# Turning the units' results by DMA in 16-bit halves, or by TensorE

## The chip, the cores and the metric

The kernel runs on one core of one Trainium2 chip. The metric is the device time of one execution in microseconds (us). Engines are named as the profile names them: PE (TensorE, the matrix engine), PEld (its weight loads), DVE (VectorE), ACT (ScalarE), POOL (GpSimd), SP (SyncE, which here only issues transfers). "SPq" is SP's queue of DMA issues. Every engine runs its instructions in the order in which they were written, and waits on semaphores for others.

## The reference

One layer of an encoder block on 2048 tokens of 1024 features, fp32 in and out:

```python
h = rms_norm(x, norm_gain)
qa, ka, va, qb, kb, vb, ga, gb, mg = split(h @ w_in)
ya = banded_attention(norm(qa) * scale, norm(ka), va, window 128, sink_a) * silu(ga)       # 8 heads of 64
yb = merge of 3 dilated groups (dilation 1, 4, 16; 8 heads of 64 each) * silu(gb)
merged = sigmoid(mg[0] + b[0]) * (ya @ w_branch_a) + sigmoid(mg[1] + b[1]) * (yb @ w_branch_b)
out = x + merged @ w_out
```

`ya` and `yb` have 512 columns each. The change concerns them after the attention, just ahead of the product with the SiLU gates.

## The kernel before, in words

Values that enter a matrix product are split in two fp16 parts (high and low) and multiplied in three products, so TensorE has three matmuls for each one of the mathematics.

**Input phase** (to about 105 us): x is normalised, split and transposed into `XH` and `XL` (features on partitions, tokens along the free dimension).

**Main phase** (about 105 to 1420 us): 14 units, 2 of kind A (4 query heads each) and 12 of kind B (2 heads of one of the three groups). A unit has 8 pairs of token blocks; the loop variable `t` counts pairs, and all offsets in the tables are in pairs (`t + 0.483` is about half a pair later). A pair's projection is two PSUM banks `pj` of 24 matmuls each (L699). ScalarE copies a bank out (`rw`, L716; `vt`, L725), VectorE reads the rest of the values (`vt`, L731), and with that the bank is free; there are two banks. Then come the norms (VectorE and POOL), a split, and a transposition by DMA into the keys' ring (`kq`, L784, on SPq). An attention item takes logits (L869), subtracts maxima (`pr`, L884 on VectorE), exponentiates (ACT), splits (`p`, L897 on ACT, L901 on VectorE), transposes the probabilities by DMA (`pt<-p`, L907 on SPq) and multiplies with the values (`pv`, L918); ScalarE copies the result out (L941, L946, L950). Between the projections stand the matmuls of the gate projections (L325).

**Merging.** When a quarter (512 tokens) of a chunk (128 columns of ya or yb) is complete, `a_merge` or `b_merge_q` writes it as `ya`, 128 tokens by 4 blocks by 128 columns in fp32, and makes a `YPart` of it. There are 8 chunks (0 to 3 from kind A, 4 to 7 from kind B) of 4 quarters, so 32 parts. A part

- `load`s the gate values `yo` from DRAM (L970),
- `turn`s the four 128x128 blocks of fp32 on TensorE, with the identity `idf` as moving operand, into the PSUM bank `pt` (L984),
- `gate`s: one VectorE instruction multiplies `pt`, a scale and `yo` (L991),
- takes the maximum (`top`, L996), and `store`s to DRAM (L999).

After quarter 3 the chunk's maximum goes over the partitions through a small matmul (`max1` to `max3`), which shares the bank `pt` with the weights' norm sums; `held` keeps the users of that bank apart.

**Last phase** (from about 1420 us): gate, branch and output projections, nearly TensorE alone.

**The order.** Nothing is reordered later. Each step is put in a heap under a planned time, `at(time, step)`, and steps are written out by rising time, so the tables of offsets (`Y_PART`, `NORM`, `LAGS`, ...) set each engine's order. `chain` runs a part's steps in their sequence and puts off one that returns False by 0.04.

Of the kernel before, what the change touches and what calls it, by code (L numbers as in the profile page):

```python
# [21 lines left out]
F32 = mybir.dt.float32  # L22
F16 = mybir.dt.float16
I32 = mybir.dt.int32
AF = mybir.ActivationFunctionType
OP = mybir.AluOpType
AX = mybir.AxisListType
# [33 lines left out]
NPAIR = 8 * NU  # L61
# [9 lines left out]
A_MERGE = (0.085, 0.258, 0.51, 0.671, 1.503, 0.761)  # L71
B_MERGE = (-0.037, 0.133, 0.333, 0.507, 0.665, 1.053)
Y_PART = (-0.097, 0.483, 0.709, 0.893, 0.943)
GATE = (-0.123, -0.064, 0.329)
W_STEP = (0.1, 0.465, 1.9, 0.445, 4.197, 0.146, 0.342)
W_MAX = (3.762, 3.892)
# [3 lines left out]
Y_FREE = 0.15  # L80
Y_MAX = (0.026, 0.815, 0.839)
# [28 lines left out]
XT_BUFS = 14  # L110
RING = 576
KQ_COPY = 0.45
V_SLOTS = 14
PT_BUFS = 4
N_BIAS_A = 384
N_BIAS_B = 256
# [2 lines left out]
def block_kernel(tc, x, w_units, w_gate, w_mrg, w_brn, w_out, w_bra, gain, qkg, sink, bias_a, bias_b, b_merge, out):  # L119
    nc = tc.nc  # L120
    V = nc.vector
    A = nc.scalar
# [7 lines left out]
    wp = es.enter_context(tc.tile_pool(name="wp", bufs=2))  # L130
    us = es.enter_context(tc.tile_pool(name="us", bufs=1))
    main = ExitStack()
    sm = main.enter_context(tc.tile_pool(name="sm", bufs=4))
    ubuf = us.tile([128, 192], F32, name="ubuf")
    ucount = [0]

    def ucol():
# [18 lines left out]
    def pow2(mx, name):  # L156
# [3 lines left out]
        p = sm.tile([128, 1], F32, name="pw_p")  # L160
        V.tensor_scalar(p[:].bitcast(I32), m[:].bitcast(I32), 0x7F800000, None, OP.bitwise_and)
        r = sm.tile([128, 1], F32, name="pw_r")
# [30 lines left out]
    held = [False, True]  # L193
# [10 lines left out]
    def norm_pow(ps):  # L204
# [5 lines left out]
        p = sm.tile([128, 1], F32, name="pw_p")  # L210
        V.tensor_scalar(p[:].bitcast(I32), m[:].bitcast(I32), -0.5, float(0x5F3759DF), OP.mult, OP.add)
        V.tensor_scalar(p[:].bitcast(I32), p[:].bitcast(I32), 0x7F800000, None, OP.bitwise_and)
        s = ucol()
# [5 lines left out]
    def w_square(u, i):  # L219
# [5 lines left out]
        c = slice(2 * i, 2 * i + 2)  # L225
        A.activation(wtiles[u][2][:, c, :n], raw[:, c, :n], AF.Square, accum_out=wtiles[u][3][:, i:i + 1])

# [11 lines left out]
    def w_hi(u, i):  # L239
        n = 384 if u < NU else 256  # L240
        raw, s, inv, wh, wl = wtiles[u]
        c = slice(2 * i, 2 * i + 2)
        A.activation(wh[:, c, :n], raw[:, c, :n], AF.Copy, scale=s[:])

# [20 lines left out]

    def rs_guess(a, n):

        y = sm.tile([128, 10], F32, name="rs_y")
        V.tensor_scalar(y[:, :n].bitcast(I32), a.bitcast(I32), -0.5, float(0x5F3759DF), OP.mult, OP.add)  # L269
        return y[:, :n]  # L270

    def rs_newton(a, yv, r, n, pool):

        t = sm.tile([128, 10], F32, name="rs_t")
        tv = t[:, :n]
        if pool:
            G.tensor_tensor(tv, yv, yv, OP.mult)  # L277
            G.tensor_tensor(tv, tv, a, OP.mult)
            G.tensor_scalar(r, tv, 0.375, -1.25, OP.mult, OP.add)
            G.tensor_tensor(r, r, tv, OP.mult)  # L280
            G.tensor_scalar(r, r, 1.875, None, OP.add)
            G.tensor_tensor(yv, r, yv, OP.mult)
            G.tensor_tensor(tv, yv, yv, OP.mult)
            G.tensor_tensor(tv, tv, a, OP.mult)
            G.tensor_scalar(tv, tv, -0.5, 1.5, OP.mult, OP.add)
            G.tensor_tensor(r, tv, yv, OP.mult)
# [58 lines left out]
    def g_square(c, i=None):  # L345
# [8 lines left out]
        k = i or 0  # L354
        A.activation(gh[:, v, :], raw[:, v, :], AF.Square, accum_out=sq[:, k:k + 1])

# [251 lines left out]
    wk = main.enter_context(tc.tile_pool(name="wk", bufs=2, reuse_waits="tile"))  # L608
# [69 lines left out]
    blocks = [0]  # L678
    vring = wk.tile([128, V_SLOTS, 2, 130], F16, name="vt", bufs=1)
    vfree = list(range(V_SLOTS))  # L680
    G.memset(vring[:, :, :, HD:HD + 1], 2.0 ** -14)

    class Pair:
# [55 lines left out]

        def stats(self):  # L740
            n = 2 * self.nh
            ss = sm.tile([128, 10], F32, name="qss")
            V.tensor_reduce(ss[:, :n], self.sq[:, :n * HD].rearrange("p (h e) -> p h e", e=HD), AX.X, OP.add)
            V.tensor_scalar(ss[:, :n], ss[:, :n], QKE / HD, self.un.eps[:], OP.mult, OP.add)
            self.ss = ss[:, :n], rs_guess(ss[:, :n], n)

        def newton(self):
            n = 2 * self.nh
            self.rr = sm.tile([128, 10], F32, name="qr")
            rs_newton(*self.ss, self.rr[:, :n], n, True)  # L750

        def scale(self):
# [208 lines left out]
    class YPart:  # L961
# [8 lines left out]
            nc.sync.dma_start(out=self.o[:], in_=gtd[self.chunk][:, 512 * self.q:512 * self.q + 512])  # L970

        def plan(self, t):
            steps = [(t + d, f) for d, f in zip(Y_PART, (self.load, self.turn, self.gate, self.top, self.store))]
            if self.q == 3:
                steps += [(t + Y_PART[3] + d, f) for d, f in zip(Y_MAX, (self.max1, self.max2, self.max3))]
            chain(steps)

        def turn(self):
            if held[0]:
                return False  # L980
            held[0] = True
            self.ps = pt_p.tile([128, 512], F32, name="pt")
            for b in range(4):
                T.transpose(self.ps[:, 128 * b:128 * b + 128], self.y[:, b, :], idf[:])  # L984

        def free(self):
            held[0] = False

        def gate(self):
            at(now[0] + Y_FREE, self.free)  # L990
            V.scalar_tensor_tensor(self.o[:], self.ps[:], gw[self.chunk][2][:], self.o[:],  # L991
                                   OP.mult, OP.mult)

# [137 lines left out]
    for u in range(NU + 1):  # L1131
        t = 8 * u
        steps = [(t + W_STEP[0] + B_GAP[0] * i, w_load, u + 1, (i,)) for i in range(4)]
# [7 lines left out]
    for c, u, slots in FILLS:  # L1141
# [4 lines left out]
        t = 8 * u  # L1146
# [5 lines left out]
    for k in range(8):  # L1152
        u = 3 + k
        t = 8 * u
# [11 lines left out]
    t = 0  # L1166
    while t < NPAIR or heap or any(k >= t for k in fill):
        u, j = divmod(t, 8)
        steps = [(f, args) for f, *args in fill.pop(t, [])]
# [23 lines left out]
        for share, f, i, args in streams:  # L1193
# [9 lines left out]
            for k, a in enumerate(after):  # L1203
                at(pos + GATE[k], a)
        until(t + .999)
# [4 lines left out]
    sm = es.enter_context(tc.tile_pool(name="sms", bufs=2))  # L1210
# [303 lines left out]
    t = clock[0]  # L1514
# [128 lines left out]
    for k, (i, q) in enumerate(steps):  # L1643
# [3 lines left out]
        p = (i // 2, q % 2)  # L1647
# [168 lines left out]
```

## Time and profile before

| what | value |
|---|---|
| median of 3 runs (range) | 1931.88 us (1931.84 to 1933.01) |
| the profiled execution, its own time | 1933.39 us |
| its span, first to last instruction | 1931.6 us |
| mean granted TensorE clock | 0.997 |
| parts `yo<-pt` on VectorE | 32, 745 ns each in the mean |
| transpositions by DMA on SPq | 256 of probabilities, 224 of keys, 12 of x |

How to read the lines that follow: in a group, "x128 | 19.2, 273 | 0.0" are the number of instructions, their busy time in us, the mean length of one in ns, and the idle time of the engine just before them, with "<-" the releaser of most of it. In a timeline a line has start and length in us, engine, line of the code, operation, out<-in, shapes, count; "[1.98 <-DVE vt L731]" is an idle stretch ahead of it and who ended it. In a list of waits: total us, number of times, longest. The 40-slice rows of the page give the busy share of each slice in tenths.

### The profile page before, as it was taken

How to read it: one execution, taken by the hardware profiler on the slowest of the kernel's cores; microseconds unless marked ns; L12 is line 12 of the kernel's file. 1: busy time of each engine (PE TensorE's matmuls, PEld its weight loads, DVE VectorE, ACT ScalarE, POOL GpSimd, SP SyncE). 2: the span in 40 equal slices, each digit the busy share in tenths (PEclk: the TensorE clock that was granted, in tenths of full speed). 3: DMA queues.
4: the chain of work that ended last, by engine and by line, in shares of the span. 5: the costliest groups of instructions: out<-in, count | busy, mean ns of one | idle time of the engine just before them, and what ended most of it. 6: DMA issues, size and time to landing. Idle time of an engine off the chain costs nothing.

```text
span 1931.6 us, 39393 instructions
## 1 busy us (share of the span) xinstructions
PE 1914.9 (99%) x13682; PEld 1209.1 (63%) x13682; DVE 1351.6 (70%) x3512; ACT 1076.4 (56%) x2454; POOL 845.5 (44%) x1849
## 2 busy tenths in 40 slices
PE   8999999999999999999999999999999999999999
PEld 6456676677766688666787667876544444444444
DVE  7568786887767777567876878768686657867322
ACT  7467666776565567565666755656444545432100
POOL 4233454344445655546555565555411210222543
PEclk9999999999999999999999999999999999999999
DMA  7449976796858596678768777766822246788763
GB/s 272 129 88 180 187 156 155 142 196 131 194 99 185 122 184 129 120 155 161 159 132 148 151 168 127 142 120 129 177 82 93 104 155 220 207 252 261 264 224 140
DMA packets 602408, 311.06 MB, mean 161 GB/s; under 512 B 470752, under 2 KB 540000, under 8 KB 600928
## 3 DMA queue, kind: packets, MB, share of 16 engines
q1 hardware_dynamic: 583776, 299.88, 66.6%
q10 hardware_dynamic: 18432, 8.66, 1.9%
q8 instruction: 107, 1.75, 0.4%
q14 instruction: 93, 0.76, 0.1%
HBM read 129.91 MB, written 65.27 MB: 101 GB/s over the span
## 4 chain that ended last, share of the span: by engine, by line
PE 92%; DVE 2%; DMA 2%; POOL 1%; ACT 1%; issue 1%; SPq 0%; DVEq 0%; POOLq 0%; ACTq 0%
PE pj L699 42%; PE fps L325 13%; PE pj L325 13%; PE fps L1683 8%; PE s L869 5%; PE fps L1478 5%; PE pv L918 4%; PE pj L599 1%; DMA xt<-in_x_dram 1%; PE pt L984 1%; DMA wraw<-in_w_units_dram 0%; DMA kq<-spl 0%; DVE rw L755 0%; DVE p L901 0%; PE pt L201 0%
## 5 line engine op out<-in xcount | busy, mean ns | idle before, releaser
L699 PE MATMUL pj<-wh,XH 128*128 128x384 f16 x1792 | 585.0, 326 | 2.0 <-DVE vt L731 2.0
L699 PE MATMUL pj<-wh,XL 128*128 128x384 f16 x1792 | 586.7, 327 | 0.0
L699 PE MATMUL pj<-wl,XH 128*128 128x384 f16 x1792 | 585.2, 327 | 0.0
L699 PEld LDWEIGHTS <-XH 128*128 128x128 f16 x3584 | 412.7, 117 | 149.7 <-issue 2.4
L884 DVE CUSTOM_DVE_ANT_0 pr<-s,b,ubuf 128x256 f32<-128x256 f32 (+3 forms) x512 | 219.3, 465 | 110.5 <-PE s L869 107.4
L699 PEld LDWEIGHTS <-XL 128*128 128x128 f16 x1792 | 207.7, 116 | 68.6
L901 DVE SCALAR_TENSOR_TENSOR p<-pr,p 128x512 f16<-128x512 f32 (+2 forms) x256 | 188.6, 737 | 23.1 <-ACT p L897 22.3
L716 ACT ACTIVATE rw<-pj 128x256 f32<-128x256 f32 (+1 forms) x224 | 87.1, 389 | 177.2 <-PE pj L699 167.1
L776 POOL COPY spl<-spl 128x256 f16<-128x256 f16 (+1 forms) x224 | 90.2, 432 | 192.3 <-DVE spl L771 190.9
L325 PEld LDWEIGHTS <-wh 128*128 128x128 f16 x960 | 93.8, 98 | 111.2 <-issue 1.2
L897 ACT ACTIVATE p<-pr 128x512 f16<-128x512 f32 (+2 forms) x256 | 159.3, 622 | 6.3
L325 PE MATMUL fps<-Y,wh 128*128 128x512 f16 x512 | 152.3, 379 | 0.0
L869 PE MATMUL s<-kq 128*128 128x256 f16 (+3 forms) x1168 | 147.9, 254 | 0.0
L918 PEld LDWEIGHTS <-pt 128*128 128x128 f16 x3024 | 125.4, 97 | 34.8
L1683 PE MATMUL fps<-wt,M 128*128 128x512 f16 (+1 forms) x684 | 145.2, 376 | 0.0
L761 POOL TENSOR_TENSOR rw<-rw,g 128x256 f32<-128x256 f32 (+1 forms) x112 | 88.9, 794 | 122.7 <-DVE rw L755 78.4
L277 POOL TENSOR_TENSOR rs_t<-rs_y 128x8 f32<-128x8 f32 (+1 forms) x112 | 38.5, 344 | 234.9 <-DVE rs_y L269 187.2
L187 POOL TENSOR_TENSOR wraw<-wraw,gn 128x768 f32<-128x768 f32 (+1 forms) x80 | 111.3, 1396 | 51.8 <-DMA wraw<-in_w_mrg_dram 43.8
L918 PE MATMUL pv<-vt,pt 128*128 128x65 f16 (+1 forms) x3024 | 132.7, 193 | 0.0
L869 PEld LDWEIGHTS <-kq 128*128 128x128 f16 x1184 | 102.0, 98 | 41.8 <-ACT kq L794 0.3
L731 DVE SCALAR_TENSOR_TENSOR vt<-pj,vt 128x128 f16<-128x128 f32 (+1 forms) x224 | 62.3, 278 | 89.3 <-ACT vt L725 88.3
L325 PE MATMUL pj<-XH,gh 128*128 128x512 f16 x320 | 121.4, 379 | 0.0
(258 smaller groups left out, 3709.5 us busy)
## 6 DMA issues: line engine op xcount, KB each, us to landing
wraw<-in_w_units_dram SPq DMA_DIRECT2D x56, 384.0 KB, 4.9
mtd<-mm SPq DMA_DIRECT2D x56, 256.0 KB, 4.0
M<-mtd SPq DMA_DIRECT2D x8, 1792.0 KB, 9.6
mgd<-fg SPq DMA_DIRECT2D x39, 256.0 KB, 2.1
zd<-z ACTq DMA_DIRECT2D x128, 66.0 KB, 2.4
zz<-zd SPq DMA_DIRECT2D x64, 132.0 KB, 2.7
xt<-in_x_dram SPq DMA_DIRECT2D x16, 512.0 KB, 8.4
gtd<-yo SPq DMA_DIRECT2D x32, 256.0 KB, 2.9
```

The source lines that it names most:

```text
L187: G.tensor_tensor(v, v, gn[:, c0:c0 + 2].unsqueeze(2).to_broadcast([128, 2, n]), OP.mult)
L325: out.append(lambda w=w, xx=xx, ch=ch, i=i: T.matmul(ps[:], lhsT=w[:, ch, c0:c0 + 128], rhs=xx[:, ch, ts], start=(i == 0), stop=(i == n - 1)))
L699: out.append(lambda lhs=lhs, rhs=rhs, ch=ch, k=k: T.matmul(ps[:, :384], lhsT=lhs[:, ch, :], rhs=rhs[:, ch, :], start=(k == 0), stop=(k == ...
L761: G.tensor_tensor(k, k, GT[un.br][:].unsqueeze(1).unsqueeze(1).to_broadcast([128, 2, un.nk, HD]), OP.mult)
L776: G.tensor_copy(sp[:, i, nh:, :, :], sp[:, i, nq:nh, ::-1, :])
L869: T.matmul(self.sv[j][:, o:o + k1 - k0], lhsT=q[:, h, qo:qo + 128], rhs=kt[:, un.nq + kh + v * un.nk, k0:k1], start=(v == 0), stop=(v == 1))
L884: V.tensor_tensor_reduce(out=self.pv[:, j, self.p0:self.p0 + W], in0=self.sv[j], in1=un.bias[:, self.h0 + j, self.b0:self.b0 + W], scale=I ...
L897: A.activation(self.sp[:, :128 * n], self.pr, AF.Copy, scale=PSC)
L901: V.scalar_tensor_tensor(self.sp[:, 128 * n:], self.pr, PSC, self.sp[:, :128 * n], OP.mult, OP.subtract)
L918: T.matmul(self.po[:, j, :w], lhsT=p[:, n * j + s, :], rhs=un.v[key][:, vh, c0:c0 + w], start=(k == 0 and s == 0), stop=(k == 2 and s == n ...
L1478: mm.append(lambda ch=ch, k=k, w=w, i=i: T.matmul(ps[:], lhsT=weight(bl, ch)[w], rhs=xblock(x, ch)[k], start=(i == 0), stop=(i == 11)))
L1683: mm.append(lambda ch=ch, k=k, w=w, i=i: T.matmul(ps[:, :cols.stop - cols.start], lhsT=m[:, a, ch, k, :], rhs=wt[w][:, b, ch, cols], start ...
```

## The change

Parts now go one of two ways. Quarters 1 and 3 of chunks 0 to 3, and the parts that are planned after the last pair (quarters 1 to 3 of chunk 7), stay as they were: 11 parts. The other 21 go over DMA: `halves` (ScalarE) writes the 16-bit halves of `ya` as two planes into `yh`; `turn_halves` (an issue on SPq) transposes the eight 128x128 blocks of 16 bits back into `ya`'s storage; `join` (ScalarE) interleaves the two planes into `yh` again, which is then read as fp32; `gate` (VectorE) reads `yh` in SBUF instead of `pt` in PSUM. `yh` has one buffer, so the next part's `halves` waits for this part's `gate`. The steps lie later than before (`Y_DMA`). Three allocations shrink: the ring of values has 12 slots instead of 14, the pool of small tiles 2 buffers instead of 4 (those of the norms keep 4), and `ubuf` 168 columns instead of 192.

```diff
 Y_PART = (-0.097, 0.483, 0.709, 0.893, 0.943)
+Y_DMA = (-0.097, 0.45, 0.55, 1.05, 1.13, 1.2, 1.25)
+Y_MAX_DMA = (0.026, 1.4, 1.45)
...
-V_SLOTS = 14
+V_SLOTS = 12
...
-    sm = main.enter_context(tc.tile_pool(name="sm", bufs=4))
-    ubuf = us.tile([128, 192], F32, name="ubuf")
+    sm = main.enter_context(tc.tile_pool(name="sm", bufs=2))
+    ubuf = us.tile([128, 168], F32, name="ubuf")
...
         def plan(self, t):
-            steps = [(t + d, f) for d, f in zip(Y_PART, (self.load, self.turn, self.gate, self.top, self.store))]
+            if t > NPAIR + 1 or self.chunk < 4 and self.q % 2:
+                end = Y_PART[3]
+                steps = list(zip(Y_PART, (self.load, self.turn, self.gate, self.top, self.store)))
+            else:
+                end = Y_DMA[5]
+                steps = list(zip(Y_DMA, (self.load, self.halves, self.turn_halves, self.join, self.gate, self.top, self.store)))
+            steps = [(t + d, f) for d, f in steps]
...
+        def halves(self):
+            self.h = wk.tile([128, 2, 512], U16, name="yh", bufs=1)
+            v = self.y.rearrange("p b c -> p (b c)").bitcast(U16).rearrange("p (c k) -> p k c", k=2)
+            A.activation(self.h[:], v, AF.Copy)
+
+        def turn_halves(self):
+            v = self.y.rearrange("p b c -> p (b c)").bitcast(U16).rearrange("p (a b) -> p a b", b=128)
+            nc.sync.dma_start_transpose(out=v, in_=self.h[:].rearrange("p k c -> p (k c)"))
+
+        def join(self):
+            v = self.y.rearrange("p b c -> p (b c)").bitcast(U16).rearrange("p (k c) -> p k c", k=2)
+            w = self.h[:].rearrange("p k c -> p (k c)")
+            A.activation(w.rearrange("p (c k) -> p k c", k=2), v, AF.Copy)
+            self.ps = w.bitcast(F32)
+
         def gate(self):
-            at(now[0] + Y_FREE, self.free)
+            if held[0] == self:
+                at(now[0] + Y_FREE, self.free)
```

How instructions move. In the rows below a line number of the changed kernel is 3 higher than before up to the class `YPart`, and 25 higher behind it.

TensorE at the first moved part (chunk 0, quarter 0), where `pj` is a projection, `s` the logits and `pt<-idf,ya` the four transpositions. Before:

```order
L869 MATMUL s<-kq 128x384
L699 LDWEIGHTS XH
L699 MATMUL pj<-wh,XH 128x384
L699 LDWEIGHTS XH
L699 MATMUL pj<-wl,XH 128x384
L984 MATMUL pt<-idf,ya 128x128 x4
L699 LDWEIGHTS XL
L699 MATMUL pj<-wh,XL 128x384
```

and after:

```order
L872 MATMUL s<-kq 128x384
L702 LDWEIGHTS XH
L702 MATMUL pj<-wh,XH 128x384
L702 LDWEIGHTS XH
L702 MATMUL pj<-wl,XH 128x384
L702 LDWEIGHTS XL
L702 MATMUL pj<-wh,XL 128x384
```

The four transpositions are gone; the projection runs through. TensorE's order is otherwise the same, but for the small matmul of the maximum of chunks 4 to 6, which stands later.

ScalarE at chunk 4, quarter 3, where `z<-pv` copies an item's result out, `rw` and `vt` empty a projection bank, `zd<-z` is a DMA issue, and `spl` splits queries and keys. Before:

```order
L796 ACTIVATE kq<-kq 128x6x64
L950 ACTIVATE z<-pv 128x2x65
L957 DMA zd_84<-z 128x132
L716 ACTIVATE rw<-pj 128x256
L725 ACTIVATE vt<-pj 128x2x64
L892 ACTIVATE pr<-pr,z 128x256 x2
L897 ACTIVATE p_10399<-pr 128x512
L950 ACTIVATE z<-pv 128x2x65
L957 DMA zd_84<-z 128x132
L767 ACTIVATE spl<-rw 128x2x4x64
```

and after:

```order
L953 ACTIVATE z<-pv 128x2x65
L1001 ACTIVATE yh<-ya 128x1024
L960 DMA zd_84<-z 128x132
L719 ACTIVATE rw<-pj 128x256
L728 ACTIVATE vt<-pj 128x2x64
L895 ACTIVATE pr<-pr,z 128x256 x2
L900 ACTIVATE p_10385<-pr 128x512
L953 ACTIVATE z<-pv 128x2x65
L960 DMA zd_84<-z 128x132
L1010 ACTIVATE yh<-ya 128x2x512
L770 ACTIVATE spl<-rw 128x2x4x64
```

`halves` (L1001) comes ahead of the bank's copy, `join` (L1010) ahead of the split that leads to the next keys.

VectorE at the same part, where `pr,z<-s` reads the logits, `p` splits the probabilities, `rw<-rw,qr` scales queries and keys, and `ym` is the chunk's maximum. Before:

```order
L991 SCALAR_TENSOR_TENSOR yo<-pt,ubuf,yo 128x512
L731 SCALAR_TENSOR_TENSOR vt<-pj,vt 128x2x64
L755 TENSOR_TENSOR rw<-rw,qr 128x512
L996 TENSOR_REDUCE ymx<-yo 128x1
L1004 TENSOR_REDUCE ym<-ymx 128x1
L1005 TENSOR_TENSOR ym<-ym 128x1
L901 SCALAR_TENSOR_TENSOR p_10399<-pr,p_10399 128x512
```

and after:

```order
L758 TENSOR_TENSOR rw<-rw,qr 128x512
L904 SCALAR_TENSOR_TENSOR p_10385<-pr,p_10385 128x512
L1016 SCALAR_TENSOR_TENSOR yo<-yh,ubuf,yo 128x512
L887 ISA pr,z<-s,b_9114,ubuf 128x192
L887 ISA z 128x1
L887 ISA pr,z<-s,b_9114,ubuf 128x192
L887 ISA z 128x1
L774 TENSOR_TENSOR spl<-rw,spl 128x2x4x64
L1021 TENSOR_REDUCE ymx<-yo 128x1
L1029 TENSOR_REDUCE ym<-ymx 128x1
L1030 TENSOR_TENSOR ym<-ym 128x1
L734 SCALAR_TENSOR_TENSOR vt<-pj,vt 128x2x64
```

Gate, maximum and the chunk's maximum move behind the next bank's `vt` read and the scaling; in their new place they stand ahead of another bank's `vt` read (L734). On SPq each of the 21 parts adds one `DMA_TRANSPOSE ya<-yh` of 8 blocks among the transpositions of probabilities and keys, and its store comes later.

More of the change, by code (lines that the diff above doesn't have):

```diff
@@ L24 @@
 I32 = mybir.dt.int32
+U16 = mybir.dt.uint16
 AF = mybir.ActivationFunctionType
@@ L266, in rs_guess @@
     def rs_guess(a, n):
-        y = sm.tile([128, 10], F32, name="rs_y")
+        y = sm.tile([128, 10], F32, name="rs_y", bufs=4)
         V.tensor_scalar(y[:, :n].bitcast(I32), a.bitcast(I32), -0.5, float(0x5F3759DF), OP.mult, OP.add)
@@ L272, in rs_newton @@
     def rs_newton(a, yv, r, n, pool):
-        t = sm.tile([128, 10], F32, name="rs_t")
+        t = sm.tile([128, 10], F32, name="rs_t", bufs=4)
         tv = t[:, :n]
@@ L741, in stats @@
             n = 2 * self.nh
-            ss = sm.tile([128, 10], F32, name="qss")
+            ss = sm.tile([128, 10], F32, name="qss", bufs=4)
             V.tensor_reduce(ss[:, :n], self.sq[:, :n * HD].rearrange("p (h e) -> p h e", e=HD), AX.X, OP.add)
@@ L748, in newton @@
             n = 2 * self.nh
-            self.rr = sm.tile([128, 10], F32, name="qr")
+            self.rr = sm.tile([128, 10], F32, name="qr", bufs=4)
             rs_newton(*self.ss, self.rr[:, :n], n, True)
@@ L972, in plan @@
         def plan(self, t):
-            steps = [(t + d, f) for d, f in zip(Y_PART, (self.load, self.turn, self.gate, self.top, self.store))]
+            if t > NPAIR + 1 or self.chunk < 4 and self.q % 2:
[5 more added lines that the diff above has]
+            steps = [(t + d, f) for d, f in steps]
             if self.q == 3:
-                steps += [(t + Y_PART[3] + d, f) for d, f in zip(Y_MAX, (self.max1, self.max2, self.max3))]
+                steps += [(t + end + d, f) for d, f in zip(Y_MAX if t > NPAIR + 1 or self.chunk < 4 and self.q % 2 else Y_MAX_DMA, (self.max1, self.max2, self.max3))]
             chain(steps)
@@ L980, in turn @@
                 return False
-            held[0] = True
+            held[0] = self
             self.ps = pt_p.tile([128, 512], F32, name="pt")
```

## Prediction

> **What bounds the kernel now.** I read the page first (span, busy shares, slices, the chain that ended last), then the waits of TensorE, then the timeline at the instructions that go, then the neighbours' rows there.
>
> ```profile
> span 1931.6 us, 39393 instructions
> PE 1914.9 (99%) x13682; PEld 1209.1 (63%) x13682; DVE 1351.6 (70%) x3512; ACT 1076.4 (56%) x2454; POOL 845.5 (44%) x1849
> ...
> PE   8999999999999999999999999999999999999999
> ...
> DVE  7568786887767777567876878768686657867322
> ...
> PE 92%; DVE 2%; DMA 2%; POOL 1%; ACT 1%; issue 1%; SPq 0%; DVEq 0%; POOLq 0%; ACTq 0%
> ```
>
> TensorE is full in every slice after the first, and 92% of the chain that ended last is its own. VectorE (70%) and ScalarE (56%) have room on average, though in the main phase VectorE stands at six to eight tenths. The waits of TensorE alone, all of them in groups of line and releaser:
>
> ```profile
> PE s L513 <- POOL xt L493: 4.0, 2, 2.5
> ...
> PE pj L699 <- DVE vt L731: 2.0, 1, 2.0
> ...
> PE fps L201 <- ACT wl L226: 0.4, 1, 0.4
> ```
>
> In the whole main phase it waits once, 2.0 us, for one read of a projection bank. So a microsecond of TensorE work that goes there is a microsecond of the span, unless a new wait eats it; and each new wait is paid in full. The question is the price of the removed work and how much lateness the neighbours bear.
>
> **The removed part: transpositions on TensorE.** Of 32 parts (8 chunks by 4 quarters) 21 move: quarters 0 and 2 of chunks 0 to 3 (8), all of chunks 4 to 6 (12), quarter 0 of chunk 7 (1). Each had 4 transpositions. Their group, and the timeline of TensorE at the first moved part:
>
> ```profile
> L984 PE MATMUL pt<-idf,ya 128*128 128x128 f32 x128 | 19.2, 273 | 0.0
> ```
> ```profile
> 183.06 0.33 PE L699 MATMUL pj<-wh,XH 128*128 128x384 f16 x1
> 183.23 0.33 PE L699 MATMUL pj<-wl,XH 128*128 128x384 f16 x1
> 183.39 0.60 PE L984 MATMUL pt<-idf,ya 128*128 128x128 f32 x4
> 183.82 0.33 PE L699 MATMUL pj<-wh,XL 128*128 128x384 f16 x1
> 183.99 0.33 PE L699 MATMUL pj<-wh,XH 128*128 128x384 f16 x1
> ```
>
> The mean of 273 ns is no price: matmuls overlap, as the projection's own rows show, which last 0.33 us and start 0.163 us apart (183.06, 183.23; 183.82, 183.99). What counts is from start to start. With the four transpositions the step from 183.23 to 183.82 is 0.59 us; without them it is 0.163. From the rounded starts one part is worth 0.43 us; unrounded it is 0.437 here, and between 0.435 and 0.473 at all 32 places. So 21 x 0.437 = 9.2 us.
>
> One of them buys nothing. Chunk 6, quarter 0:
>
> ```profile
> 1109.91 0.60 PE L984 MATMUL pt<-idf,ya 128*128 128x128 f32 x4
> ...
> 1110.67 0.33 PE L699 MATMUL pj<-wh,XL 128*128 128x384 f16 x1
> 1112.97 0.32 PE L699 MATMUL pj<-wh,XH 128*128 128x384 f16 x1 [1.98 <-DVE vt L731]
> ```
>
> This is the one wait of the main phase. Without the transpositions TensorE is there 0.44 us sooner and waits that much longer. That leaves 20 x 0.437 = 8.75, about 8.8 us.
>
> The Trainium skill, page "TensorE: Matmul & The Clock Gate", section "Part 4: PE-mode transpose", gives about 275 ns for a transposition in one kernel's context. The length of the row (273) agrees, the spacing (109) doesn't price it so; by the page the 84 that go would be worth 84 x 0.275 = 23.1 us. I follow the spacing.
>
> **The added part on ScalarE: two copies per part.** `halves` and `join` each pass 1024 elements of 16 bits per partition, one with a step of two elements on the read, one on the write. No row before has 16-bit integers in such steps. Nearest rows:
>
> ```profile
> L473 ACT ACTIVATE jk<-xt 128x1024 f16<-128x1024 f32 x16 | 16.9, 1057 | 2.9 <-DMA xt<-in_x_dram 2.6
> ...
> L796 ACT ACTIVATE kq<-kq 128x384 f16<-128x384 f16 x16 | 8.2, 512 | 3.9 <-DMA kq<-spl 3.9
> ```
>
> Between 384 elements of 16 bits (0.51 us) and 1024 from 32 bits (1.06) lie 0.85 ns for each further element, the same rate for both widths, so I take 1.06 each. Ends: 0.5, if 16-bit elements went in pairs, which the row of 384 does not show, and 2.1, if the step doubled the price of each. 21 x 2 x 1.06 = 44.5 us on an engine that is busy 56% of the span. What hides it is this:
>
> ```profile
> L716 ACT ACTIVATE rw<-pj 128x256 f32<-128x256 f32 (+1 forms) x224 | 87.1, 389 | 177.2 <-PE pj L699 167.1
> ```
>
> ScalarE stands 167 us in all waiting for TensorE to finish a projection bank: it is early at most of the 224 reads. If that cover is gone, 1 us late on ScalarE meets the bank's margin, below.
>
> **The added transposition by DMA and its in-order queues.** On SyncE's queue each of the 21 issues is one more 8-block transposition; the rows of the same kind:
>
> ```profile
> L907 SPq DMA_TRANSPOSE pt<-p x256: 1188/1242/2666, 115.3 to 1385.1; - x128
> ...
> DMA to landing us min/median/max: 2.4/3.6/7.3
> ```
>
> 1.24 us of the queue and 3.6 us to landing (2.4 to 7.3 as ends). Behind the issue stand the transpositions of the probabilities and of the keys. Where the issue comes to the head of the queue before `halves` is done, the queue stands up to 2 us more. `join` waits for the landing on ScalarE, `gate` for `join` on VectorE. The tightest of the 21 are the last quarters of chunks 4, 5 and 6, where halves, issue, join and gate lie closest. Chunk 4's, before:
>
> ```profile
> 682.28 0.26 ACT L950 ACTIVATE z<-pv 128x130 f32<-128x130 f32 x1
> ...
> 684.58 0.38 ACT L716 ACTIVATE rw<-pj 128x256 f32<-128x256 f32 x1 [2.03 <-PE pj L699]
> ...
> 686.72 0.28 ACT L950 ACTIVATE z<-pv 128x130 f32<-128x130 f32 x1
> ...
> 687.40 0.63 ACT L767 ACTIVATE spl<-rw 128x512 f16<-128x512 f32 x1 [0.40 <-ACT z L950]
> 689.17 0.38 ACT L716 ACTIVATE rw<-pj 128x256 f32<-128x256 f32 x1 [1.14 <-PE pj L699]
> ...
> 693.77 0.38 ACT L716 ACTIVATE rw<-pj 128x256 f32<-128x256 f32 x1 [0.98 <-PE pj L699]
> ```
> ```profile
> 684.58 0.75 DVE L991 SCALAR_TENSOR_TENSOR yo<-pt,ubuf,yo 128x512 f32<-128x512 f32 x1
> 685.24 0.28 DVE L731 SCALAR_TENSOR_TENSOR vt<-pj,vt 128x128 f16<-128x128 f32 x1
> ...
> 687.02 0.69 DVE L901 SCALAR_TENSOR_TENSOR p<-pr,p 128x512 f16<-128x512 f32 x1
> 688.36 0.42 DVE L884 CUSTOM_DVE_ANT_0 pr<-s,b,ubuf 128x192 f32<-128x192 f32 x1 [0.65 <-PE s L869]
> ...
> 689.76 0.29 DVE L731 SCALAR_TENSOR_TENSOR vt<-pj,vt 128x128 f16<-128x128 f32 x1
> ```
> ```profile
> 683.05 1.28 SPq L907 DMA_TRANSPOSE pt<-p  x1
> ...
> 690.22 2.55 SPq L784 DMA_TRANSPOSE kq<-spl  x2
> ```
>
> `halves` goes behind the first L950 and ends near 683.6 inside the idle 2.03 us. The issue then starts at 683.6 (the row at 683.05 moves behind it and is 1.8 late), and lands near 687.2. `join` stands behind the second L950, so ScalarE waits 0.2 and is done at 688.3; L767 starts 0.9 late and the 1.14 of idle time takes that up before L716 at 689.17. `gate` stands behind L901, which ends at 687.71: VectorE waits till 688.3 and gives 0.75 to the gate, so L884 is 0.7 late; the maximum over the part then follows, and L731 at 689.76 ends near 691.7 where it ended at 690.05. Its bank is wanted again when the other one is full, which the next L716 dates to 693.77: 2 us are left. TensorE does not wait. The keys at 690.22 issue at most 1 us late; the second of the two lands 3.2 us after its issue in the median and the product that needs it comes at 697.16:
>
> ```profile
> 697.16 0.60 PE L869 MATMUL s<-kq 128*128 128x256 f16 x4
> ...
> DMA to landing us min/median/max: 2.7/3.2/6.4
> ```
>
> 691.5 + 3.2 = 694.7, so 2.4 us are to spare, 1.4 after the change. In the other 18 parts the pieces lie further apart, and the same count leaves more. The gate itself reads SBUF on both sides now:
>
> ```profile
> L901 DVE SCALAR_TENSOR_TENSOR p<-pr,p 128x512 f16<-128x512 f32 x136 | 103.9, 764 | 18.7 <-ACT p L897 18.2 <-issue 0.3
> ...
> L991 DVE SCALAR_TENSOR_TENSOR yo<-pt,ubuf,yo 128x512 f32<-128x512 f32 x32 | 23.8, 745 | 5.7 <-PE pt L984 3.9 <-DMA yo<-gtd 1.9
> ...
> L1247 DVE SCALAR_TENSOR_TENSOR Y<-yg,ubuf,Y 128x512 f16<-128x512 f32 x12 | 10.9, 914 | 3.5 <-ACT Y L1244 3.5
> ```
>
> 0.69 to 0.91 in place of 0.745, off the path: 0.
>
> Other edits at nothing: 12 value slots for 14 (a free slot is still there at each take, and the read of the bank that fills it follows the old reader on TensorE); 2 buffers for 4 in the small pool (their users are one engine or a unit apart); a later store and maximum (read only after the main phase). The bank `pt` is no longer held by moved parts, which can only ease the norm sums. The DMA engines get 21 transpositions more beside the 256 of that row and those of the keys.
>
> For landings longer than the median and the units' tight starts I allow 0.5 us (ends: 0, and 5 as reckoned for rival one). Span 1931.6 - 8.8 + 0.5 = 1923.3. The profiled execution took 1933.39 with that span, the median of the runs is 1931.88, 0.08% less; taking the difference from the median gives 1931.9 - 8.3 = 1923.6.
>
> **Rivals.** (1) Part of it is given back: the three chunk ends and the units' starts lose 1 to 2 us each to VectorE waiting for `join`, where landings take 5 rather than 3.6. Three ends at 1.5 and a few of 0.2 make 3 to 6 us: 1926 to 1928.5. For it speaks that VectorE is at eight tenths there; against it the 2 us left above.
> (2) Slower: every landing takes the longest time shown, 7.3 us, since more transpositions share the path. Then `join` comes 2.4 to 4.8 us late in eight parts (those with 0.9 to 4.9 us between issue and join's place), ScalarE and VectorE stand still, and beyond a margin of 2 us, plus the copy of 1.06, TensorE loses 1.4 to 3.8 in each: about 21 us, 1931.9 - 8.8 + 21 = 1944. It decides from some 5.5 us of landing on. The median over 256 such transfers speaks against it. The Trainium skill, page "VectorE: DVE Perf Modes", section "Rules for kernel authors", advises TensorE for a 128x128 transposition if a PSUM destination is fine, and DMA otherwise, which speaks against this change. No row before compares the two on one tile, and TensorE alone is full here; I give the rule no more than this case.
> (3) The removed rows count at their length, as if nothing overlapped: 84 x 0.273 = 22.9, 1909. The start-to-start spacing speaks against it. (The page's price of 275 ns would come to the same.)
> (4) Nothing comes of it: the gaps fill with waits as at 1110.67, everywhere. 1931.9. Against it: that wait is the only one of the main phase.
>
> **How the numbers follow.** Forecast 0.72 (its own range 1921.5, if the 2.0 us wait shrinks too, to 1925.5); rival one 0.11, two 0.06, three 0.03, four 0.08. Range 1921.5 to 1928.5 holds the forecast and rival one, 0.83. A change within 0.2% (3.9 us) can hardly be told from none: faster 0.86 (forecast, one, three), same 0.08, slower 0.06.
>
> **What would show it.** 44 transpositions of `ya` on TensorE in place of 128; the step over a moved place 0.163 us; `halves` and `join` rows near 1.06 us; landings of `ya` near 3.6; TensorE's waits no longer than some 4 us in the main phase, the one near 1100 still there. I am wrong if new waits of TensorE behind VectorE's L731 or for keys appear at the chunk ends, or the copies take 2 us.

## The result, and the profile after

| | before | after |
|---|---|---|
| median (range) | 1932.41 us (1929.94 to 1933.77) | 1927.42 us (1925.9 to 1929.43), 12 runs |
| ratio, 95% interval | | 0.9976 (0.9967 to 0.9985) |
| the profiled execution, its span | 1933.39, 1931.6 | 1929.07, 1927.3 |

The median before is that of 12 runs, one of which took 2514.68 us and is left out of the range; without it the median is 1932.29 us. The change gains 5.0 us by the medians in the table, 4.3 by the two spans. 8.3 were forecast. The page after (span, busy times, and the engines' shares of the chain that ended last):

```profile
span 1927.3 us, 39322 instructions
...
PE 1907.4 (99%) x13598; PEld 1200.4 (62%) x13598; DVE 1359.2 (71%) x3512; ACT 1121.3 (58%) x2496; POOL 850.0 (44%) x1849
...
PE 87%; DVE 4%; DMA 3%; POOL 2%; issue 2%; ACT 2%; SPq 0%; DVEq 0%; POOLq 0%; ACTq 0%
```

TensorE has 84 matmuls less and is as full as before, but its share of the chain fell from 92% to 87%. What that is worth the shares do not tell (e7, below, has 88% with half of the waits); the waits of TensorE do. Those that are new or changed (total us, times, longest):

```profile
PE pt L204 <- DVE yo L1016: 2.1, 2, 1.1
...
PE pj L702 <- DVE vt L734: 1.6, 2, 1.3
PE s L872 <- DMA kq<-spl: 1.5, 2, 1.3
```

Together 5.2 us in the main phase, where before there was one wait of 2.0. The first row is the norm sum of a chunk's maximum (`norm_sum`, the product of `ym` with ones), which wants the bank `pt` that a gate (`yo`, L1016) still reads. The second is a projection bank read late, the third keys that have not landed.

The new path by its tile `yh` (min/median/max ns), and what its engines waited for:

```profile
L1001 ACT ACTIVATE yh<-ya x21: 1040/1048/1058, 183.7 to 1350.4; 128x1024 uint16<-128x1024 uint16 x21
L1005 SPq DMA_TRANSPOSE ya<-yh x21: 1231/1232/2289, 188.9 to 1355.7; - x21
L1010 ACT ACTIVATE yh<-ya x21: 1338/1350/1392, 193.1 to 1359.2; 128x1024 uint16<-128x1024 uint16 x21
L1016 DVE SCALAR_TENSOR_TENSOR yo<-yh,ubuf,yo x21: 737/751/1643, 196.3 to 1360.6; 128x512 f32<-128x512 f32 x21
its engine sat idle before it (us, times) until:
  ACT yh L1010: 16.7, 11
...
DMA to landing us min/median/max: 3.0/3.4/5.5
```

VectorE stood still for the join (L1010) in 11 of the 21 parts, 16.7 us in all. TensorE's timeline where the first moved part was:

```profile
183.57 0.33 PE L702 MATMUL pj<-wl,XH 128*128 128x384 f16 x1
183.73 0.33 PE L702 MATMUL pj<-wh,XL 128*128 128x384 f16 x1
```

The step over the place is 0.16 us, where it was 0.59.

**One wait followed back.** TensorE, then VectorE, in after, near 284 us:

```profile
282.96 0.49 PE L872 MATMUL s<-kq 128*128 128x192 f16 x4
284.54 0.38 PE L204 MATMUL pt<-ym,ones 128*128 128x1 f32 x2 [1.09 <-DVE yo L1016]
```
```profile
269.58 1.64 DVE L1016 SCALAR_TENSOR_TENSOR yo<-yh,ubuf,yo 128x512 f32<-128x512 f32 x1 [1.87 <-ACT yh L1010]
...
283.75 0.74 DVE L1016 SCALAR_TENSOR_TENSOR yo<-pt,ubuf,yo 128x512 f32<-128x512 f32 x1
```

The gate at 283.75 belongs to a part that was not moved (chunk 1, quarter 3) and holds the bank. The same gate before:

```profile
283.06 0.74 DVE L991 SCALAR_TENSOR_TENSOR yo<-pt,ubuf,yo 128x512 f32<-128x512 f32 x1
```

It stood 0.7 us earlier, although TensorE was 1.4 us later than now: the norm sum began at 284.67, 0.33 us behind the logits' row, and the same distance behind the row at 282.96 is 283.3. Ahead of the late gate on the same engine, 14 us earlier, stands the moved gate at 269.58: that one waited 1.87 us for the join and then took 1.64 us in place of 0.75. From there to 283.75 VectorE idles 0.8 us in all, so it cannot make that up. Why 1.64 shows in the rows of ScalarE and GpSimd:

```profile
268.20 1.35 ACT L1010 ACTIVATE yh<-ya 128x1024 uint16<-128x1024 uint16 x1
```
```profile
269.63 1.05 POOL L1066 TENSOR_TENSOR ya<-zz,am_e 128x512 f32<-128x512 f32 x1 [1.31 <-ACT yh L1010]
```

GpSimd's next product waits for the same join, since the join reads the buffer `ya` that the product will fill. So gate and product are let go together. That happens at four of the 21 parts: at three the gate takes 1.64 us and the product 1.05, at the fourth it is the other way round:

```profile
429.69 0.75 DVE L1016 SCALAR_TENSOR_TENSOR yo<-yh,ubuf,yo 128x512 f32<-128x512 f32 x1 [1.71 <-ACT yh L1010]
```
```profile
429.74 1.61 POOL L1066 TENSOR_TENSOR ya<-zz,am_e 128x512 f32<-128x512 f32 x1 [0.95 <-ACT yh L1010]
```

The other 18 moved gates take at most 0.79 us, and no gate of the kernel before, which read PSUM and one tile of SBUF, took more than 0.75. The Trainium skill, page "SBUF — State Buffer", section "Who interferes with whom", says that a VectorE instruction with two SBUF inputs contends with a GpSimd instruction that reads SBUF, and that the order of issue decides who blocks. One of the two being longer at all four places agrees; by the records the gate began first each time, and three times it was the longer one.

### The profile page after: what moved, and what is told of

The parts are those of the page before. It is cut to its first block, busy times and chain, and to the rows that moved or that the text cites. A ratio compares the mean times of both kernels' runs of the same rounds, so it can differ in the third digit from the quotient of the medians.

```text
span 1927.3 us, 39322 instructions
## 1 busy us (share of the span) xinstructions
PE 1907.4 (99%) x13598; PEld 1200.4 (62%) x13598; DVE 1359.2 (71%) x3512; ACT 1121.3 (58%) x2496; POOL 850.0 (44%) x1849
## 4 chain that ended last, share of the span: by engine, by line
PE 87%; DVE 4%; DMA 3%; POOL 2%; issue 2%; ACT 2%; SPq 0%; DVEq 0%; POOLq 0%; ACTq 0%
PE pj L702 38%; PE fps L328 13%; PE pj L328 12%; PE fps L1708 8%; PE s L872 5%; PE fps L1503 5%; PE pv L921 4%; PE pj L602 2%; DMA kq<-spl 1%; DVE qss L746 0%; DVE pr L887 0%; POOL xt L496 0%; DVE p L904 0%; DVE rw L758 0%; DMA b<-in_bias_a_dram 0%
## 5 line engine op out<-in xcount | busy, mean ns | idle before, releaser
L904 DVE SCALAR_TENSOR_TENSOR p<-pr,p 128x512 f16<-128x512 f32 (+2 forms) x256 | 190.1, 743 | 21.5 <-ACT p L900 20.6
L758 DVE TENSOR_TENSOR rw<-rw,qr 128x512 f32<-128x512 f32 (+1 forms) x112 | 103.9, 928 | 32.6 <-POOL qr L289 31.7
L734 DVE SCALAR_TENSOR_TENSOR vt<-pj,vt 128x128 f16<-128x128 f32 (+1 forms) x224 | 62.2, 278 | 88.6 <-ACT vt L728 87.9
```

The source lines that it names most:

```text
L758: V.tensor_tensor(q, q, self.rr[:, :n].unsqueeze(2).to_broadcast([128, n, HD]), OP.mult)
L904: V.scalar_tensor_tensor(self.sp[:, 128 * n:], self.pr, PSC, self.sp[:, :128 * n], OP.mult, OP.subtract)
```

## Experiments

Theory: the 21 parts free 9.2 us on TensorE, and some 4 come back because VectorE, which works in order, stands at the join, so that gates, bank reads and keys behind it come late. Rivals: the path's own work on ScalarE, SyncE and the DMA engines; a TensorE that merely runs into deadlines; the allocations. "Waits" is the sum of the three kinds of waits shown above (bank `pt`, values `vt`, keys `kq`) in the profiled run. "From 1st projection" is the profiled run's time from the start of the first projection matmul to the end of its span. What lies ahead of that start is the input phase, which no edit here changes and which alone took between 75.5 and 77.5 us in these 14 runs. So this column tells kernels apart that the medians of a few runs can't, but it rests on one run each. The rows for before and after, whose spans are 1931.6 and 1927.3 (minimum, median and longest duration in ns, then the first and the last start in us):

```profile
L699 PE MATMUL pj<-wh,XH x1792: 322/326/364, 77.2 to 1350.0; 128*128 128x384 f16 x200
```
```profile
L702 PE MATMUL pj<-wh,XH x1792: 322/326/363, 77.5 to 1345.6; 128*128 128x384 f16 x200
```

| kernel | parts | median us | ratio to before, 95% | waits us | from 1st projection, us |
|---|---|---|---|---|---|
| before | 0 | 1932.3 to 1932.6 | 1 | 2.0 | 1854.4 |
| after | 21 | 1927.42 | 0.9976 (0.9967 to 0.9985) | 5.2 | 1849.8 |
| e1, path left out | 21 | 1922.44 | 0.9950 (0.9937 to 0.9964) | 1.3 | 1844.7 |
| e2, path and TensorE | 21 | 1934.36 | 1.0008 (0.9999 to 1.0017) | 2.7 | 1855.9 |
| e3, norm sum later | 21 | 1925.89 | 0.9963 (0.9950 to 0.9975) | 4.2 | 1848.2 |
| e4, chunks 4 to 7 alone | 13 | 1928.20 | 0.9976 (0.9967 to 0.9986) | 2.1 | 1849.2 |
| e5, gate waits for no join | 21 | 1923.86 | 0.9957 (0.9944 to 0.9971) | 3.4 | 1848.4 |
| e6, norm sum earlier | 21 | 1926.54 | 0.9973 (0.9963 to 0.9983) | 4.2 | 1848.0 |
| e7, join later | 21 | 1923.49 | 0.9957 (0.9944 to 0.9969) | 2.6 | 1846.1 |
| e8, three edits | 21 | 1925.22 | 0.9966 (0.9954 to 0.9979) | 3.5 | 1846.9 |
| e9, join earlier | 21 | 1926.80 | 0.9972 (0.9961 to 0.9984) | 2.6 | 1847.1 |
| e10, join later, all parts | 29 | 1931.63 | 0.9999 (0.9990 to 1.0008) | 9.9 | 1850.9 |
| e11, join later, norm sum earlier | 21 | 1924.68 | 0.9959 (0.9945 to 0.9972) | 3.0 | 1846.5 |
| e12, allocations alone | 0 | 1932.71 | 1.0001 (0.9992 to 1.0009) | 2.3 | 1854.6 |

(The norm sum's waits are counted by any releaser, `yo`, `wm` or `gh`; in e12 0.4 for ScalarE's copy into `kq`.)

**e1: what the path costs at all.** `halves`, `turn_halves` and `join` go, and a moved gate reads the untransposed tile:

```
+ direct: self.ps = self.y; self.gate()
- zip(Y_DMA, (load, halves, turn_halves, join, gate, top, store))
+ zip(Y_DMA[:1] + Y_DMA[4:], (load, direct, top, store))
```

> The 21 moved parts are neither split, transposed nor joined: the gate reads the untransposed product from SBUF (the transposition is left out), at the place where it stands in the kernel after. So TensorE saves what it saves there and ScalarE, SyncE and the DMA path do nothing for it. Theory (the 21 parts are worth 9.2 us, some 4 of which come back because VectorE waits for the join and later instructions on it come late): the waits of the norm sum at about 283 and 501 us go, the time is 9 us under before, 1923 to 1924. Rival (TensorE only runs into deadlines that VectorE and the keys set anyway, whatever the new path costs): the same waits stay, 4 to 5 us under before, about 1927.

```profile
PE pj L702 <- DVE vt L734: 1.3, 1, 1.3
```

This is the only one of the three kinds left (the old wait near 1100). 10.2 us under before by the medians, 9.7 from the first projection on: the theory's 9, though the median lies 0.6 us below the 1923 to 1924 expected, and not the rival's 4 to 5. TensorE's freed time is real, and without the path nearly all of it reaches the end (9.2 us, and 0.7 by which the old wait is shorter). So the path gives 5 us back (5.0 by the medians, 5.1 from the first projection on).

**e2: the path without a faster TensorE.** `halves` to `join` as in after, and four transpositions into `pt` for each moved part as well:

```
+ extra, planned at 0.44: held[0] = self; ps = pt_p.tile(...); 4 x T.transpose(ps[...], self.y[:, b, :], idf[:])
```

> The moved parts take the DMA path, and TensorE still transposes them too, into the bank pt that nobody then reads (128 transpositions as before). Theory (split, join and transposition cost nothing by themselves; only a TensorE that comes earlier meets them): within 1 us of before, since TensorE is then no earlier than before. Rival (the new work on ScalarE, SyncE and VectorE costs 4 us by itself, whatever TensorE does): 4 us above before, about 1936.

```profile
PE pt L204 <- DVE yo L1025: 1.5, 2, 0.8
...
PE pj L702 <- DVE vt L734: 0.8, 1, 0.8
...
PE s L872 <- DMA kq<-spl: 0.4, 1, 0.4
```

1.8 us over before, interval -0.2 to 3.3, and 1.5 from the first projection on: between theory and rival. The norm sum waits although TensorE is as slow as before, so the waits are not only a TensorE that comes earlier; VectorE is late by itself. The old wait near 1100 is 0.8 us here, where before had 2.0 with the same work on TensorE: there VectorE's new order helps.

**e3: move the waiting norm sum.** `Y_MAX` of chunks 0 to 3 replaced by `Y_MAX_DMA`, whose second step is 1.4.

> Kernel after, with the norm sum of chunks 0 to 3 planned later (1.4 in place of 0.815 behind the maximum, as for the moved parts), so that it is no longer the instruction right behind the gate that frees its bank. Theory (two waits on the bank pt, 1.25 and 1.21 us, are part of what was given back): those two waits go and the time is 2.0 to 2.5 us under after, about 1925. Rival (TensorE then meets VectorE at the next value or key instead): no change, 1927.4.

```profile
PE pj L702 <- DVE vt L734: 3.1, 2, 1.8
...
PE s L872 <- DMA kq<-spl: 1.1, 2, 0.7
```

The norm sum's waits are gone (no such row), but a wait of 1.8 us for values `vt` stands near 302 us where 0.3 had been. 1.5 us under after by the medians, whose intervals overlap, and 1.6 from the first projection on. The lateness of VectorE is passed on, as the rival said, and part of it is gained.

**e4: the parts of chunks 4 to 7 alone.** The condition `self.chunk < 4 and self.q % 2` becomes `self.chunk < 4`.

> Only the 13 parts of chunks 4 to 7 take the DMA path, the 8 of chunks 0 to 3 are transposed on TensorE again. Theory (those 8 bring 8 x 0.437 = 3.5 us and lose 3.1 in the waits at 283, 304 and 501): within 0.7 us of after, and the waits at 283 and 501 are gone. Rival (every part brings the same share, 5 us over 21): 1.9 us above after, about 1929.3.

```profile
PE pj L702 <- DVE vt L734: 1.3, 1, 1.3
...
PE s L872 <- DMA kq<-spl: 0.8, 1, 0.8
```

Same ratio as after, with 8 parts less, and no norm sum waits. In the kernel after, those 8 parts bring almost nothing: they are priced at 3.5 us and the medians differ by 0.8. By the medians the 0.7 of the theory and the 1.9 of the rival are both within the uncertainty; from the first projection on e4 is 0.6 us shorter than after, which speaks for the theory.

**e5: the path stays, VectorE does not wait for it.**

```
+ src = self.o if hasattr(self, "h") else self.ps
- V.scalar_tensor_tensor(self.o[:], self.ps[:], ...
+ V.scalar_tensor_tensor(self.o[:], src[:], ...
```

> Split, transposition and join are all issued as in the kernel after, at the same places, but the gate of a moved part reads its own gate tile in place of the joined product, so VectorE waits for no join (the product is left out of the output for those parts). Theory (what is given back comes from VectorE standing in order behind the join): near the kernel that left the path out, 1922.4 us, so 1922 to 1924, and no wait of the norm sum at 283 and 501 us. Rival (ScalarE's and SyncE's time for the path, or the later maximum, does it): 1926 to 1928, the waits stay.

1923.86 us, 3.6 under after: the theory's range. All copies, issues and transfers of the path are still there, so most of what was given back comes through the gate's tie to the join (the wait, and the lengthening beside GpSimd's product that comes with it), not from the work of the path. Against the expectation one norm sum still waits, 2.1 us at 497 us; VectorE there stood for the load of an unmoved gate, which was issued at 493.4 and landed at 498.5:

```profile
DVE yo L1017 <- DMA yo<-gtd: 2.5, 1, 2.5
```

From the first projection on this run is 3.7 us longer than e1's. All of it lies in the stretch of the one unit with that wait: 2.1 us are the wait itself, 1.6 a slow clock behind it (last section). Over every other unit's projections the two agree within 0.1 us. It was the slowest of e5's five runs, the others being 1.2 to 3.0 us faster; whether they had the wait is not known.

**e6: the later maximum.** `Y_MAX_DMA = (0.026, 0.55, 0.574)`.

> Kernel after, but the norm sum of chunks 4 to 6 stands 0.55 behind the maximum in place of 1.4, which is where it stood before the change in the unit's time; chunks 0 to 3 as in after. Theory (the later norm sum put eight small VectorE instructions, 1.1 us, ahead of the keys of the next unit, which TensorE waits for at 975 us for 1.44): the wait at 975 goes and the time is 0.8 to 1.4 us under after, 1926 to 1926.6. Rival (the slow issue of those keys, 3.83 us against 2.54, is all of that wait and differs from run to run): no change in the median, 1927.4.

```profile
PE pt L204 <- DVE yo L1016: 2.0, 2, 1.0
...
PE pj L702 <- DVE vt L734: 1.8, 2, 1.3
PE s L872 <- DMA kq<-spl: 0.4, 1, 0.4
```

The wait for keys at 975 is gone from the profile, and from the first projection on it is 1.8 us shorter than after, but the median fell by 0.9 us only, with ratios that can't be told apart. The slow issue alone does not make the wait: here it took 3.69 us, nearly the 3.83 of after, and nothing waited. Nor does the later norm sum alone: e4 has it too, and no wait at 975. That the two together made it is not shown.

**e7: the join later.** Join to store 0.13 of a pair later:

```
- Y_DMA = (-0.097, 0.45, 0.55, 1.05, 1.13, 1.2, 1.25)
+ Y_DMA = (-0.097, 0.45, 0.55, 1.18, 1.26, 1.33, 1.38)
```

`Y_MAX_DMA` becomes (0.026, 1.27, 1.32), so those norm sums stay.

> Kernel after, with join, gate, maximum and store of the moved parts 0.13 of a pair (0.6 us) later. Theory (VectorE waits 16.7 us in 11 places for the join; later places cut that by 0.6 us each): those waits under 12 us, the norm sum's waits at 283 and 501 shorter by some 0.5 each, 1926 to 1927. Rival (VectorE's order is only shifted, and what stands behind is as late as before): 1927.4 or 0.5 above.

VectorE's wait for the join, TensorE's waits, and the gate that was followed above:

```profile
DVE yo L1016 <- ACT yh L1010: 2.2, 4, 0.9
```
```profile
PE pj L702 <- DVE vt L734: 1.8, 2, 1.4
...
PE pt L204 <- DVE yo L1016: 0.6, 1, 0.6
...
PE s L872 <- DMA kq<-spl: 0.2, 1, 0.2
```
```profile
266.96 0.88 DVE L904 SCALAR_TENSOR_TENSOR p<-pr,p 128x512 f16<-128x512 f32 x1
267.77 1.53 DVE L1016 SCALAR_TENSOR_TENSOR yo<-yh,ubuf,yo 128x512 f32<-128x512 f32 x1
```

16.7 us of VectorE's waits became 2.2; at the gate shown, work that was ready (L904) now stands ahead of it. The time is 3.9 us under after (3.7 from the first projection on), more than the 0.4 to 1.4 expected, and level with e5, where VectorE waits for no join at all. It is the fastest of the kernels that compute the whole result.

**e8: three edits together.** e7's places, the norm sums of chunks 0 to 3 at 1.1 and those of chunks 4 to 6 at 0.42.

> The last three edits together: chunks 0 to 3 with the norm sum at 1.1 in place of 0.815, chunks 4 to 6 with theirs where it stood before the change, join and gate 0.13 of a pair later. Theory: the gains add up to about 3 us over after, 1924 to 1925. Rival (each moved place opens the next wait, as at 300 us in the kernel with the late norm sum): 1925.5 to 1926.5, no better than that one edit.

```profile
PE pj L702 <- DVE vt L734: 2.4, 2, 1.3
PE pt L204 <- DVE wm L211: 1.1, 2, 0.9
```

The rival by its mechanism, with a median between the two ranges: moving the norm sums as well brings back waits at 302 and 503 us, and it is no better than e7.

**e9: the join earlier.** `Y_DMA = (-0.097, 0.45, 0.55, 0.92, 1.0, 1.07, 1.12)`.

> The other direction: join, gate, maximum and store of the moved parts 0.13 of a pair (0.6 us) earlier than in the kernel after (norm sums of chunks 4 to 6 at the same place). Theory (what is lost is set by how long VectorE and ScalarE stand at the join): VectorE's waits for the join rise from 16.7 us in 11 places to 25 or more, TensorE's waits grow by 3 us or more, 1930 to 1933. Rival (the gain of the later join was not due to its wait): 1926 to 1928.

VectorE's wait and ScalarE's, then TensorE's:

```profile
DVE yo L1016 <- ACT yh L1010: 17.6, 13, 2.4
```
```profile
ACT yh L1010 <- DMA ya<-yh: 22.6, 12, 3.1
```
```profile
PE pj L702 <- DVE vt L734: 1.4, 1, 1.4
PE s L872 <- DMA kq<-spl: 1.2, 3, 0.7
```

A miss for the theory: no slower than after. ScalarE took the longer wait for the transfer (9.8 us before this edit), VectorE's rose by 0.9 only, the norm sums' waits vanished, and no moved gate is lengthened now (the longest is 0.77 us). So how long VectorE stands in all does not give the time. What the traces point to is how late it is where TensorE next wants something. The gate that was followed above had both in after, a wait of 1.87 us and 0.9 us of lengthening; e7 has only the lengthening there, e9 only a wait of 1.32 us, and the norm sum behind it waits in neither. From the first projection on, e9's profiled run is 2.7 us shorter than after's and 1.0 longer than e7's. By the medians it is 0.6 shorter and 3.3 longer; part of that is the input phase, which took 1.6 us more in e9's profiled run than in e7's. The other runs of e9 have no trace.

**e10: more parts.** e7's places, and quarters 1 and 3 of chunks 0 to 3 as well.

> The later join (0.13 of a pair), and all quarters of chunks 0 to 3 take the DMA path: 29 parts moved in place of 21. Theory (a part is worth 0.437 us once VectorE does not wait for its join): 8 x 0.437 = 3.5 us under the kernel with the later join, 1920 to 1921. Rival (the units of chunks 0 to 3 have no room left on VectorE and ScalarE): 1923 or above.

```profile
PE pj L702 <- DVE vt L734: 7.5, 6, 2.2
...
PE pt L204 <- ACT gh L358: 1.6, 2, 1.0
```
```profile
DVE yo L1016 <- ACT yh L1010: 9.5, 11, 3.2
```

The rival: by the medians all is lost. 29 parts are worth 12.7 us on TensorE, and the ratio is 0.9999. The profiled run, the fastest of the eleven and 1.5 us under the median, lost 9.9 us in these kinds of waits; from the first projection on it is 3.5 us under before, but 4.8 over e7, so the 8 further parts cost more than they free. The busy shares do not show why: between 60 and 500 us, the units of chunks 0 to 3, VectorE is busy 76% of the time, as in before, and ScalarE 71% (64% in before).

**e11 and e12.** e7 with the norm sums of chunks 4 to 6 at 0.42; and the allocations with all parts on TensorE, in the order of the kernel before.

> The later join (0.13 of a pair) and the norm sums of chunks 4 to 6 where they stood before the change. Theory (keys late at a unit's start are the next wait): 0.3 to 0.8 us under the kernel with the later join, 1922.7 to 1923.3. Rival (no wait for keys above 0.4 us is left in that kernel): the same, 1923.5.

> Only the allocations of the change (12 value slots, the small pool at 2, the narrower buffer of columns); all 32 parts on TensorE, its order as in before. Theory (the allocations cost nothing): ratio 1.000 within 0.001. Rival (part of what is missing was paid for the space): 1 to 3 us above before.

e11 can't be told from e7: the rival. e12 is 1.0001 (0.9992 to 1.0009): the allocations cost nothing.

## Why the prediction was right, and where not

1927.4 lies in the range, 3.8 us above the forecast and outside the forecast's own 1921.5 to 1925.5, in the band given to rival one. So the range held because it took in a rival with a chance of 0.11; the forecast's own account, in which nothing new holds TensorE up, did not. The signs that it named say the same: TensorE waits 5.2 us in these rows where some 4 were the limit, and new waits behind L734 and for keys came (at 304 and 975 us), though not at the ends of chunks 4 to 6. Its steps:

- **A part is worth 0.437 us, 21 of them 9.2: right.** e1 shows it best: 9.7 us from the first projection on, of which 0.7 is the shorter old wait. The runs scatter with the granted clock: of the runs of before beside the experiments, 21 at 0.998 have a mean of 1931.4 us, 25 at 0.997 1932.9. In the traces that difference lies in the input phase, where the clock of the first 77 us is 0.93 in before, 0.91 in after and 0.96 in e7; from 77 to 1350 us it is 1.00 in all three. At 0.998, e1's mean is 1922.4 (3 runs), 9.0 less than before. At the same clock after has 1926.6 (3 runs), 4.8 less.
- **Rivals three and four (22.9 us, and nothing): wrong,** by the same runs. The long wait, which was to grow by one part's 0.44 us, shrank from 2.0 to 1.3; in e1 it is 1.3 as well. So the one part that was taken to buy nothing did count.
- **Copies of 1.06 us: half right.** The split is 1.048, the join, which writes with a step of two elements, 1.350.
- **Issue 1.24, landing 3.6 (at most 7.3): right,** 1.232 and 3.4, at most 5.5. The point of rival two, landings of 5.5 in general, was not reached. (Its figures do not fit together: with 0.9 us between issue and join's place a landing of 7.3 makes the join 6.4 us late, not at most 4.8.)
- **The tightest places, the last quarters of chunks 4 to 6: right that TensorE does not wait.** VectorE's wait was put at 0.6 us in the worked place and is 2.15, mostly because it got there earlier:

```profile
688.10 0.75 DVE L1016 SCALAR_TENSOR_TENSOR yo<-yh,ubuf,yo 128x512 f32<-128x512 f32 x1 [2.15 <-ACT yh L1010]
...
691.03 0.29 DVE L734 SCALAR_TENSOR_TENSOR vt<-pj,vt 128x128 f16<-128x128 f32 x1
```

  The bank read at 691 ends at 691.3; 691.7 was reckoned.
- **"In the other 18 parts the pieces lie further apart, and the same count leaves more": wrong.** One part was worked out and taken for the tightest. VectorE waited in 11 parts, and the places that paid were those near 284, 304 and 502 us, where parts of chunks 0 to 3 are gated or have just been, and one unit's start at 975 us.
- **"The bank `pt` is no longer held by moved parts, which can only ease the norm sums": the step that failed.** The unmoved parts of the same units still hold it, and their gates stand on VectorE behind the moved ones. Cost 0 was set; 2.1 us is in the row.
- **The allowance of 0.5 us: mis-sized.** The waits rose by 3.2 us in the profiled run, and by the medians the gain is 8.8 - 5.0 = 3.8 us less than the sum without the allowance. Against e1 5.0 us are missing.
- **The gate at 0.69 to 0.91, off the path: wrong in three parts,** where it took 1.64 beside GpSimd's product. That the join keeps the buffer `ya`, and so holds that product back, was not seen.
- **Allocations 0: right** (e12). **The later maximum 0:** not decided (e6).
- **Rival one** had the mechanism (VectorE waiting for the join) and the size, but put it at the chunk ends and behind landings of 5 us. It came at the places just named, with landings of 3.4 in the median: 4.8 ahead of the gate at 269.58, but 3.1 ahead of the one at 488.54, the next that held up a norm sum. Its "eight tenths" for VectorE are 7, 8 and 8 at the three chunk ends, and the main phase runs from five to eight tenths; nothing hangs on that.
- **TensorE or DMA for a transposition.** 21 parts came out 5 us faster by DMA on a kernel whose TensorE is full; with 29 parts, by the medians, nothing is gained. The Trainium skill, page "VectorE: DVE Perf Modes", section "Rules for kernel authors", advises TensorE where a PSUM destination is fine. For these 21 parts that does not hold (1927.42 us by DMA, 1932.41 by TensorE).

Shown: the path gives back 5 us (e1), and most of it goes through the gate's tie to the join, on VectorE (e5, e7); in e5's profiled run all but one place is as fast as without the path. The total of VectorE's waits is not the measure (e9). Open: why one load landed late in e5, and why e9's median is 3.3 us over e7's when its profiled run has the same 2.6 us of waits.

## What to carry to other kernels

Work freed on the full engine pays only if the replacement's last step does not make another engine's in-order queue late where the full engine wants a result. Place the consumer behind work that is ready, rather than at the moment when the transfer is due (0.6 us of planned delay was worth 3.9 us here), and try the other direction too: 0.6 us earlier gained 2.7 us in its one profiled run, 0.6 by the medians. When an engine's lateness is judged, follow what stands behind it to the next point at which the full engine wants a result, also for work that the change does not touch. A few rows of slack against one place do not speak for the others; 8 more parts in the first units cost 4.8 us from the first projection on. And where kernels differ by a few us, compare them from a point behind the phases that the change leaves alone: here those phases alone scatter by 2 us.

## What the runs showed of the hardware

- A copy of 1024 16-bit elements per partition on ScalarE takes 1048 ns with a step of two on the read, 1350 ns with a step of two on the write.
- TensorE's granted clock fell once after a short wait. In e5, after 2.1 us without work that ended at 499.5:

```profile
495.00:500.00 5.00, 2.90 (x26) 2.41 (x25) 2.38 (x6) 2.55 (x6) 3.16 (x13) 1.00 1.02 235
500.00:503.30 3.30, 3.30 (x13) 1.84 (x12) 2.76 (x15) 2.23 (x8) 0.18 (x1) 0.55 1.09 260
```

  (Windows of the span; the third number from the end is the clock.) Matmuls of the projection then start 0.32 us apart in place of 0.16 for 3 us, which costs 1.6 us on top of the wait. The wait of 2.0 us near 1111 us in the kernel before left the clock at 1.00. The Trainium skill, page "TensorE: Matmul & The Clock Gate", section "Part 1: The HAM clock gate", gives half the clock after an idle window of about 3.4 us. This wait was shorter; the 3.3 us of the slow stretch are near the length of that window.
